# Seven-product up-projections summed in their PSUM banks, three down-products side by side, two plain pairs first

## Chip, cores and metric

The kernel runs on one core of a Trainium2 chip. The metric is the device time of one execution in microseconds (us); three executions of the kernel before gave 2522.79, 2525.11 and 2525.51, median 2525.11.

## What is computed

Two blocks of a transformer-like network on 512 tokens of width 1024, all in float32: sparse attention (A), a squared-ReLU MLP (M0), an RWKV-7 mixer (B), a second MLP (M1), a norm, a SwiGLU stage (S1), a convolution and mLSTM mixer (C), and a SwiGLU stage (S2). The change touches only M0 and M1:

```
def sqrelu_mlp(h, w_up, w_down):        # w_up 1024 x 4096, w_down 4096 x 1024
    u = jax.nn.relu(h @ w_up)
    return (u * u) @ w_down
...
x = x + sqrelu_mlp(rms_norm(x, mlp_norm[i]), mlp_w_up[i], mlp_w_down[i])
```

## The kernel before

Activations lie transposed: eight tiles of 128 features by 512 tokens (`self.x`). To keep float32 accuracy every operand is split in two: a rounded part `hi` (ScalarE, a cast) and the rest `lo` (VectorE, a subtraction), and every product is three matmuls, hi·hi, hi·lo and lo·hi (`mm3`, L452 to L456). A weight unit is 128 output features of 1024 inputs. `Weights` fetches raw tiles with SyncE's DMA queue (`wraw`, three buffers), and splits them in halves of 128 x 512 (`whi`, `wlo`). `ahead` splits as many halves as there are free buffers; a buffer is free once the products that used it have been written down, so the place of a call of `ahead` in the program settles what stands in ScalarE's and VectorE's queues at that point. Every engine works through its own queue in the order in which the program names the instructions (`manual_schedule`).

`mlp` (L568 to L626) goes through 32 blocks of hidden features in four groups of eight. A group first makes its eight blocks in four pairs (up-projection, ReLU times the norm's factor `rs`, square, split into `uh` and `ul`), then eight down-products, each over the group's eight blocks, each added to a tile of x (L624).

The first pair of all is plain: `product` with n=2, 48 matmuls of 512 columns in k = 0 to 7, six for each k. All other pairs are made by `product7` (L513): a Winograd form of Strassen's method on 2 x 2 blocks (two feature blocks by two halves of 256 tokens, the inputs in two halves of four tiles), with seven products P1 to P7 of 12 matmuls of 256 columns, 84 in all. Its inputs are P1, P2, P3 on the activations themselves and P4 to P7 on sums of them, made once for each MLP by `sums` (L485 to L511, four calls, q = 0 to 3). The sums of weights are made in place on VectorE (L170 to L177). The seven products of a pair lie in four of six PSUM banks, and ScalarE (L537) and VectorE (L538 to L545) join them into the four quarters of the output. The weights of a pair are split in the order P1, P7, P2, P6, P5, P3, P4, and the products run in that order too.

Beside the first plain pair run `stats_beside` (after k = 4 the sums of squares go through TensorE and the inverse root through ScalarE and VectorE; after k = 6 four transposes spread it, L436, and L438 copies it to `rs`) and the four calls of `sums` (after k = 1, 2, 3 and 5, L595 to L598).

Weight buffers: six halves for plain halves and P1, P2, P3 of the sevens, and six more for P4 to P7. In what follows the pairs of a group are called first to fourth.

## Time and profile before

| | |
|---|---|
| median of three runs | 2525.11 us |
| profiled execution, its own time | 2521.3 us |
| its span, first to last instruction | 2519.5 us |
| TensorE (PE) busy | 2307.1 us, 92% |
| VectorE (DVE) busy | 1610.8 us, 64% |
| ScalarE (ACT) busy | 1070.6 us, 42% |
| M0's products | from 274.0 to 668.1 us of the span |
| M1's products | from 1121.9 to 1517.9 us of the span |

In a timeline row stand the start in us, the duration, the engine, the line, the operation, the tiles out<-in with their shapes, and in brackets how long the engine was idle before and what ended that. PE's matmuls overlap, so the time one really takes is the distance to the next one's start. In a group's row stand the count, the busy time, the mean ns of one, and the idle time of the engine just before them. PEclk is the share of TensorE's clock that was granted.

### The profile page before, as it was taken

To read this page: it belongs to the slowest core of one execution; us is meant where nothing else is said; L and a number is where in the kernel's file an instruction comes from. 1 tells how busy PE (TensorE), PEld (TensorE's weight loads), DVE (VectorE), ACT (ScalarE), POOL (GpSimd) and SP (SyncE) were. 2 spreads that over 40 slices of the span, in tenths; PEclk is the share of its full clock that TensorE was granted. 3 is DMA by queue.
4 is the path that set the end of the run, shared out by engine and by line. 5 is a ranking of instruction groups with operands and counts; after the bars stand their busy time and mean duration, and the time that the engine had idled before them with its cause. 6 is when DMAs were issued, how large, how long until landed. Compare 5 with 4: busy or idle time off the path is not lost. (4 is left out here: it accounts for less than half of the span.)

```text
span 2519.5 us, 36278 instructions
## 1 busy us (share of the span) xinstructions
PE 2307.1 (92%) x13900; PEld 1930.3 (77%) x13900; DVE 1610.8 (64%) x2865; ACT 1070.6 (42%) x1967; POOL 424.9 (17%) x430
## 2 busy tenths in 40 slices
PE   7889788988988799887988989999998998999997
PEld 6668678878766676776878877888887787788886
DVE  7987757657688964777657665444457764634445
ACT  5566434334466365434334343333235544333222
POOL 3754000000355532220000020000012102100002
PEclk9999899999988898998999999999998999999999
DMA  4320222222323357532222222323222322222222
GB/s 157 94 80 19 70 89 93 89 87 86 119 64 118 101 169 204 164 101 68 92 84 92 93 84 93 100 92 101 92 74 74 111 76 76 92 92 93 100 95 65
DMA packets 105853, 241.97 MB, mean 96 GB/s; under 512 B 18120, under 2 KB 36936, under 8 KB 105680
## 3 DMA queue, kind: packets, MB, share of 16 engines
q1 hardware_dynamic: 103488, 234.46, 29.3%
q0 software_dynamic: 1040, 3.51, 0.4%
q8 instruction: 110, 1.80, 0.3%
q10 hardware_dynamic: 1152, 1.68, 0.2%
q14 instruction: 63, 0.52, 0.1%
HBM read 214.62 MB, written 19.22 MB: 93 GB/s over the span
## 5 line engine op out<-in xcount | busy, mean ns | idle before, releaser
L454 PE MATMUL mm<-xh,whi 128*128 128x512 f32 (+3 forms) x2080 | 742.9, 357 | 18.8 <-ACT whi L241 7.2
L456 PE MATMUL mm<-xh,wlo 128*128 128x512 f32 (+3 forms) x2080 | 733.6, 353 | 11.0 <-DVE wlo L242 11.0
L455 PE MATMUL mm<-xl,whi 128*128 128x512 f32 (+3 forms) x2080 | 734.1, 353 | 9.1 <-DVE xl L364 8.0
L242 DVE TENSOR_TENSOR wlo<-wraw,whi 128x512 fp32r<-128x512 f32 (+3 forms) x582 | 436.7, 769 | 405.7 <-ACT whi L241 404.5
L241 ACT CAST whi<-wraw 128x512 fp32r<-128x512 f32 (+2 forms) x601 | 355.1, 611 | 456.5 <-PE mm L455 398.0
L454 PEld LDWEIGHTS mm<-xh,whi 128*128 128x128 f32 (+2 forms) x2080 | 399.6, 192 | 78.0 <-issue 12.9
L456 PEld LDWEIGHTS mm<-xh,wlo 128*128 128x128 f32 (+2 forms) x2080 | 398.2, 191 | 66.7 <-DVE wlo L242 14.6
L455 PEld LDWEIGHTS mm<-xl,whi 128*128 128x128 f32 (+2 forms) x2080 | 399.4, 192 | 64.6 <-DVE xl L364 14.1
L454 PE MATMUL mm<-uh,whi 128*128 128x512 f32 (+1 forms) x900 | 356.0, 396 | 49.2 <-ACT uh L588 49.2
L455 PE MATMUL mm<-ul,whi 128*128 128x512 f32 (+1 forms) x900 | 355.3, 395 | 4.2 <-DVE ul L589 4.2
L456 PE MATMUL mm<-uh,wlo 128*128 128x512 f32 (+1 forms) x900 | 353.2, 392 | 0.0
L380 POOL TENSOR_TENSOR acc<-acc,sq 128x512 f32<-128x512 f32 (+1 forms) x55 | 73.5, 1337 | 1534.6 <-ACT sq L379 1534.2
L454 PEld LDWEIGHTS mm<-uh,whi 128*128 128x128 f32 x900 | 173.9, 193 | 90.4 <-ACT uh L588 52.7
L455 PEld LDWEIGHTS mm<-ul,whi 128*128 128x128 f32 x900 | 173.6, 193 | 47.1 <-DVE ul L589 9.2
L456 PEld LDWEIGHTS mm<-uh,wlo 128*128 128x128 f32 x900 | 173.5, 193 | 37.5
L230 ACT CAST whi<-wraw 128x512 fp32r<-128x512 f32 x180 | 107.3, 619 | 126.8 <-PE mm L455 43.2
L232 DVE TENSOR_TENSOR wlo<-wraw,whi 128x512 fp32r<-128x512 f32 x180 | 121.8, 686 | 26.0 <-ACT whi L230 23.7
L624 DVE TENSOR_TENSOR x<-mm,x 128x512 f32<-128x512 f32 x64 | 44.3, 691 | 69.8 <-PE mm L456 69.8
L589 DVE TENSOR_TENSOR ul<-u,uh 128x1024 fp32r<-128x1024 f32 x32 | 39.2, 1226 | 68.1 <-ACT uh L588 68.1
L587 ACT ACTIVATE u<-t 128x1024 f32<-128x1024 f32 x32 | 33.9, 1059 | 108.6 <-DVE t L610 102.8
L363 ACT ACTIVATE xh<-x,vec 128x512 fp32r<-128x512 f32 (+1 forms) x50 | 35.2, 705 | 87.3 <-DVE x L624 23.7
L772 ACT CAST uh<-a 128x512 fp32r<-128x512 f32 x44 | 27.3, 621 | 76.2 <-DVE a L771 76.2
(538 smaller groups left out, 3244.8 us busy)
## 6 DMA issues: line engine op xcount, KB each, us to landing
wraw<-in_ffn_in SPq DMA_DIRECT2D x88, 512.0 KB, 3.8
wraw<-in_up SPq DMA_DIRECT2D x64, 512.0 KB, 4.1
wraw<-in_down SPq DMA_DIRECT2D x64, 512.0 KB, 3.8
wraw<-in_rwkv SPq DMA_DIRECT2D x34, 512.0 KB, 4.9
wraw<-in_ffn_out SPq DMA_DIRECT2D x32, 512.0 KB, 3.7
wraw<-in_mix SPq DMA_DIRECT2D x32, 512.0 KB, 3.8
wraw<-in_dsa SPq DMA_DIRECT2D x23, 512.0 KB, 3.9
wraw<-in_ffn_out SPq DMA_DIRECT2D x16, 384.0 KB, 3.0
```

What stands on the lines that cost most here:

```text
L230: self.nc.scalar.copy(hi, t)
L232: self.nc.vector.tensor_sub(lo, t, hi.bitcast(F32))
L241: self.nc.scalar.copy(hi[:, :per], t)
L242: self.low.tensor_sub(lo[:, :per], t, hi[:, :per].bitcast(F32))
L363: nc.scalar.activation(hi, x, AF.Copy, scale=gm)
L380: (low or (nc.vector if m == NB - 1 else nc.gpsimd)).tensor_add(acc, acc, q[:, s])
L454: nc.tensor.matmul(ps, w[0], x[0], start=start, stop=False)
L455: nc.tensor.matmul(ps, w[0], x[1], start=False, stop=False)
L456: nc.tensor.matmul(ps, w[1], x[0], start=False, stop=stop)
L587: nc.scalar.activation(u, t, AF.Square)
L589: nc.vector.tensor_sub(lo, u, hi.bitcast(F32))
L624: nc.vector.tensor_add(self.x[m], p, self.x[m])
```

## The change

Three edits in M0 and M1.

1. `product7` now uses two PSUM banks and lets products go on in a bank in which others have been summed: the first half of bank a takes P1, then P6, P7 and P4 on top, bank x takes P2 in its first half and P5, then P3, in its second. ScalarE copies the sum out between (four copies, L535, L540, L543, L546 of the changed kernel), VectorE makes the rest (L608, L617) and the ReLUs (L600). The products run as P1, P2, P6, P5, P7, P3, P4; the weights are still split in the old order. The squares are made for each block of 128 x 512 by itself (L594, L595, L597).
2. The second pair of each MLP is plain too. Its `sums` run after k = 7 of the first pair (q = 0) and after k = 1, 3, 5 of the second.
3. The first three down-products of each group run side by side, three matmuls of each for every k.

```diff
--- before.py
+++ after.py
@@ -449,11 +449,11 @@
                 nc.vector.scalar_tensor_tensor(self.x[m], self.x[m], self.v(first, m), r1, op0=OP.mult, op1=OP.mult)
 
 
-    def mm3(self, ps, w, x, start, stop):
+    def mm3(self, ps, w, x, start, stop, **how):
         nc = self.nc
-        nc.tensor.matmul(ps, w[0], x[0], start=start, stop=False)
-        nc.tensor.matmul(ps, w[0], x[1], start=False, stop=False)
-        nc.tensor.matmul(ps, w[1], x[0], start=False, stop=stop)
+        nc.tensor.matmul(ps, w[0], x[0], start=start, stop=False, **how)
+        nc.tensor.matmul(ps, w[0], x[1], start=False, stop=False, **how)
+        nc.tensor.matmul(ps, w[1], x[0], start=False, stop=stop, **how)
 
     def product(self, xs, cols=128, n=1, pool=None, hook=None):
 
@@ -510,40 +510,49 @@
                           (("P5", 0, first), ("P4", 0, s), ("P6", 1, first), ("P7", 1, s))}
         return sums
 
-    def product7(self, xg, out):
+    def product7(self, xg, put):
 
 
         nc = self.nc
         at = self.w.get_seven()
-        banks = [self.mmp.tile([128, T], F32, name="mm") for _ in range(4)]
-        u2, u = self.c7.tile([128, 1, 256], F32, name="u2"), self.c7.tile([128, 2, 256], F32, name="u43")
+        a, x = (self.mmp.tile([128, T], F32, name="mm") for _ in range(2))
+        plus, c22 = (self.c7.tile([128, T], F32, name=n) for n in ("c1", "c2"))
         first, s = HALVES
-        P = dict(P1=banks[0][:, first], P2=banks[0][:, s], P6=banks[1][:, first], P5=banks[2][:, first],
-                 P7=banks[2][:, s], P3=banks[3][:, first], P4=banks[3][:, s])
-        two = [b.rearrange("p (i t) -> p i t", i=2) for b in banks]
-        C = out.rearrange("p (i t) -> p i t", i=4)
-        v = nc.vector
         self.w.ahead()
-        for p in SPLIT_ORDER:
+
+        def run(p, out, start):
+
             hi, lo = self.w.half(at[p])
             for q in range(NB // 2):
                 xs = {"P1": (q, first), "P2": (q + 4, first), "P3": (q + 4, s)}.get(p)
                 xs = [t[:, xs[1]] for t in xg[xs[0]]] if xs else self.x7[q][p]
                 c = slice(q * 128, (q + 1) * 128)
-                self.mm3(P[p], (hi[:, c], lo[:, c]), xs, q == 0, q == NB // 2 - 1)
+                self.mm3(out, (hi[:, c], lo[:, c]), xs, start and q == 0, q == NB // 2 - 1, skip_group_check=True)
             self.w.release(at[p])
-            if p == "P2":
-
-                nc.scalar.copy(u2[:, 0], P["P1"])
-                v.tensor_add(C[:, 0], u2[:, 0], P["P2"])
-            elif p == "P6":
-                v.tensor_add(u2[:, 0], u2[:, 0], P["P6"])
-            elif p == "P5":
-                v.tensor_add(u, u2.to_broadcast([128, 2, 256]), two[2])
-                v.tensor_add(C[:, 3], u[:, 1], P["P5"])
-            elif p == "P4":
-                v.tensor_add(C[:, 1:3], u, two[3])
-            self.w.ahead()
+
+        a, b, c = a[:, first], x[:, first], x[:, s]
+        run("P1", a, True)
+        nc.scalar.copy(plus[:, first], a)
+        self.w.ahead()
+        run("P2", b, True)
+        self.w.ahead()
+        run("P6", a, False)
+        nc.scalar.copy(plus[:, s], a)
+        self.w.ahead()
+        run("P5", c, False)
+        nc.scalar.copy(c22[:, first], c)
+        self.w.ahead()
+        run("P7", a, False)
+        nc.scalar.copy(c22[:, s], a)
+        put(1, 1, c22[:, first], c22[:, s])
+        self.w.ahead()
+        run("P3", c, False)
+        put(0, 0, x, plus)
+        self.w.ahead()
+        run("P4", a, False)
+        put(1, 0, a, None)
+        self.w.ahead()
+        put(2, 0, None, None)
 
     def part(self, p, w, c, x, s, k, K, free):
 
@@ -572,44 +581,63 @@
             self.stp = st.enter_context(tc.tile_pool(name="st_m", bufs=1, space=PSUM))
             self.sqp = st.enter_context(tc.tile_pool(name="sq_m", bufs=2))
             self.pad(st)
-            up = st.enter_context(tc.tile_pool(name="u_m", bufs=G // 2 + 1))
+            up = st.enter_context(tc.tile_pool(name="u_m", bufs=G + 2))
             self.pad(st)
-            tp = st.enter_context(tc.tile_pool(name="t_m", bufs=1))
+            tp = st.enter_context(tc.tile_pool(name="t_m", bufs=2))
             xg = self.xg
             st7 = ExitStack()
             sums = self.open_seven(st7)
 
-            def two():
-                return [tp.tile([128, 2 * T], F32, name=n) for n in "tu"]
-
-            def unit(t, u):
-                hi, lo = (up.tile([128, 2 * T], F32R, name=n) for n in ("uh", "ul"))
+            def square(t):
+                u = tp.tile([128, T], F32, name="u")
+                hi, lo = (up.tile([128, T], F32R, name=n) for n in ("uh", "ul"))
+                nc.scalar.activation(hi, t, AF.Square)
                 nc.scalar.activation(u, t, AF.Square)
-                nc.scalar.activation(hi, t, AF.Square)
-                nc.vector.tensor_sub(lo, u, hi.bitcast(F32))
-                us.extend((hi[:, i * T:(i + 1) * T], lo[:, i * T:(i + 1) * T]) for i in range(2))
+                us.append((hi, lo))
+                return lambda: nc.vector.tensor_sub(lo, u, hi.bitcast(F32))
+
+            def relu(t, p, s=ALL):
+                nc.vector.scalar_tensor_tensor(t[:, s], p, 0.0, self.rs[:, s], op0=OP.max, op1=OP.mult)
+
+            def put(i, h, p, plus):
+
+                if i == 2:
+                    later.pop()()
+                    return
+                if i and h:
+                    nc.vector.tensor_add(plus, p, plus)
+                    later.append(tp.tile([128, T], F32, name="t"))
+                    relu(later[0], plus, HALVES[1])
+                elif i:
+                    relu(later[0], p, HALVES[0])
+                    t, low = later
+                    later[:] = [square(t)]
+                    low()
+                else:
+                    nc.vector.tensor_add(plus, p, plus)
+                    t = tp.tile([128, T], F32, name="t")
+                    relu(t, plus)
+                    later.append(square(t))
 
             def beside(k):
                 self.stats_beside(k)
-                if k in (1, 2, 3, 5):
-                    sums(min(k - 1, 3), self.vec[:, VCOL[gn]:VCOL[gn] + NB], lambda: [t[:, :T] for t in two()])
+                if k == 7:
+                    sums_at(0)
+
+            def sums_at(q):
+                sums(q, self.vec[:, VCOL[gn]:VCOL[gn] + NB], lambda: [tp.tile([128, T], F32, name=n) for n in "tu"])
 
             for g in range(nff // G):
-                us = []
+                us, later = [], []
                 for f in range(0, G, 2):
-                    if g == 0 and f == 0:
-                        ps = self.product(xg, n=2, hook=beside)
-                        t, u = two()
-                        for i, p in enumerate(ps):
-                            nc.vector.scalar_tensor_tensor(t[:, i * T:(i + 1) * T], p, 0.0, self.rs,
-                                                           op0=OP.max, op1=OP.mult)
+                    if g == 0 and f < 4:
+                        ps = self.product(xg, n=2, hook=(beside, lambda k: k in (1, 3, 5) and sums_at(k // 2 + 1))[f // 2])
+                        for p in ps:
+                            t = tp.tile([128, T], F32, name="t")
+                            relu(t, p)
+                            square(t)()
                     else:
-                        t, u = two()
-                        self.product7(xg, t)
-                        t2 = t.rearrange("p (i t) -> p i t", i=2)
-                        nc.vector.scalar_tensor_tensor(t2, t2, 0.0, self.rs[:, None, :].to_broadcast([128, 2, T]),
-                                                       op0=OP.max, op1=OP.mult)
-                    unit(t, u)
+                        self.product7(xg, put)
                 last = g == nff // G - 1
                 if last:
                     self.w.close_seven()
@@ -619,8 +647,10 @@
                     self.xg_pool = None
                 if last and nxt:
                     blk = nxt()
+
+                ps = self.product(us, n=3)
                 for m in range(NB):
-                    p, = self.product(us)
+                    p = ps[m] if m < 3 else self.product(us)[0]
                     nc.vector.tensor_add(self.x[m], p, self.x[m])
                     if last and nxt:
                         blk(m)
@@ -2177,9 +2207,9 @@
     def f(aps):
         r = []
         for g in range(4):
-            r += [(aps[f"up{i}"][g * 4 + j], [1024, 1024], ["seven" if g + j else None] * 2) for j in range(4)]
+            r += [(aps[f"up{i}"][g * 4 + j], [1024, 1024], ["seven" if g or j > 1 else None] * 2) for j in range(4)]
             r += [(aps[f"down{i}"][g * 4 + j], [1024, 1024]) for j in range(4)]
-        return r, ([2] * 4 + [1] * 8) * 4
+        return r, ([2] * 4 + [3] + [1] * 5) * 4
     return f
 
 
```

The tables that follow show where instructions went. Names are those of the tiles; a number that tells two buffers apart is left in some.

**Beside the first plain pair, VectorE.** L497 to L506 are one call of `sums`, L389 to L399 the inverse root of the statistics, L438 the copy to `rs`. Before:

```order
L497 SCALAR_TENSOR_TENSOR t<-x_74,ng,t 128x256
L499 SCALAR_TENSOR_TENSOR u<-x_78,vec,t 128x512
L501 SCALAR_TENSOR_TENSOR t<-x_78,vec,u 128x256
L506 TENSOR_TENSOR xl_3081<-t,xh_3080 128x512
L506 TENSOR_TENSOR xl_3085<-u,xh_3084 128x512
L389 TENSOR_SCALAR sv<-st 128x4
L396 RECIPROCAL sy<-sy 128x4
L397 SCALAR_TENSOR_TENSOR stt<-sy,sv 128x4
L398 TENSOR_TENSOR stt<-stt,sy 128x4
L399 SCALAR_TENSOR_TENSOR sy<-stt,sy 128x4
L497 SCALAR_TENSOR_TENSOR t<-x_75,ng,t 128x256
```

Now:

```order
L242 TENSOR_TENSOR wlo<-wraw,whi 128x512 x3
L389 TENSOR_SCALAR sv<-st 128x4
L396 RECIPROCAL sy<-sy 128x4
L397 SCALAR_TENSOR_TENSOR stt<-sy,sv 128x4
L398 TENSOR_TENSOR stt<-stt,sy 128x4
L399 SCALAR_TENSOR_TENSOR sy<-stt,sy 128x4
L438 COPY rs<-st 128x512
L491 TENSOR_SCALAR ng<-vec 128x8
L497 SCALAR_TENSOR_TENSOR t<-x_72,ng,t 128x256
```

The inverse root stood behind three calls of `sums`; now it stands ahead of all four.

**Second plain pair to the first `product7` of an MLP, ScalarE, now.** L505 are the casts of the last call of `sums`, L594 and L595 the squares of the second plain pair, and L535 is the copy of P1 of the first `product7`:

```order
L496 ACTIVATE t<-x_75,vec 128x256
L505 CAST xh_3212<-t 128x512
L505 CAST xh_3216<-u 128x512
L594 ACTIVATE uh<-t 128x512
L595 ACTIVATE u<-t 128x512
L594 ACTIVATE uh<-t 128x512
L595 ACTIVATE u<-t 128x512
L230 CAST whi<-wraw 128x512
L230 CAST whi<-s_3255 128x512
L535 COPY c_3250<-mm 128x256
```

The copy comes next in that queue behind this piece, after one cast of `wraw` and one of `s`; before, no matmul waited for it.

**First to second pair of the second group, ScalarE.** L537 is the copy of P1 before, L535 now; L230 are casts of weights, L587 and L588, now L594 and L595, the squares of the first pair. Before:

```order
L537 COPY u_3883<-mm 128x256
L230 CAST whi<-wraw 128x512 x4
L230 CAST whi<-s_3979 128x512
L587 ACTIVATE u<-t 128x1024
L588 ACTIVATE uh<-t 128x1024
L230 CAST whi<-wraw 128x512 x2
L537 COPY u_4024<-mm 128x256
```

Now:

```order
L535 COPY c_3845<-mm 128x256
L540 COPY c_3845<-mm 128x256
L543 COPY c_3846<-mm 128x256
L546 COPY c_3846<-mm 128x256
L230 CAST whi<-wraw 128x512 x6
L594 ACTIVATE uh<-t 128x512
L595 ACTIVATE u<-t 128x512
L594 ACTIVATE uh<-t 128x512
L595 ACTIVATE u<-t 128x512
L230 CAST whi<-s_3943 128x512
L535 COPY c_3993<-mm 128x256
```

In both the copy of the second pair's P1 stands behind the squares of the first pair. Now it is also what P6, the third product of that pair, has to wait for, since P6 goes on in the bank of P1.

**The same place, VectorE.** L170 to L177 are sums of weights, L232 the `lo` parts. Before:

```order
L177 TENSOR_TENSOR wraw<-wraw,s_3856 128x512
L232 TENSOR_TENSOR wlo<-wraw,whi 128x512 x2
L538 TENSOR_TENSOR t<-u_3883,mm 128x256
L540 TENSOR_TENSOR u_3883<-u_3883,mm 128x256
L232 TENSOR_TENSOR wlo<-wraw,whi 128x512
L170 TENSOR_TENSOR wraw<-wraw 128x512
L232 TENSOR_TENSOR wlo<-wraw,whi 128x512
L542 TENSOR_TENSOR u_3884<-u_3883,mm 128x512
L543 TENSOR_TENSOR t<-u_3884,mm 128x256
L232 TENSOR_TENSOR wlo<-wraw,whi 128x512
L173 TENSOR_TENSOR s_3979<-wraw 128x512
L232 TENSOR_TENSOR wlo<-wraw,whi 128x512
```

Now (L608 and the L600 under it follow on P7 of the first pair, L617 and the L600 under it make the first block that the squares wait for):

```order
L608 TENSOR_TENSOR c_3846<-c_3846 128x256
L600 SCALAR_TENSOR_TENSOR t<-c_3846,rs 128x256
L177 TENSOR_TENSOR wraw<-wraw,s_3822 128x512
L232 TENSOR_TENSOR wlo<-wraw,whi 128x512 x3
L170 TENSOR_TENSOR wraw<-wraw 128x512
L232 TENSOR_TENSOR wlo<-wraw,whi 128x512 x2
L173 TENSOR_TENSOR s_3943<-wraw 128x512
L232 TENSOR_TENSOR wlo<-wraw,whi 128x512
L617 TENSOR_TENSOR c_3845<-mm,c_3845 128x512
L600 SCALAR_TENSOR_TENSOR t<-c_3845,rs 128x512
L600 SCALAR_TENSOR_TENSOR t<-mm,rs 128x256
L597 TENSOR_TENSOR ul<-u,uh 128x512
```

Nine instructions on weights, for the second and the third pair, now stand in one run between the first pair's P7 and L617; before, they were spread over its products.

## Rows read from the trace of the kernel before

**Rows 1.** The page: engines (busy, share, count), and one costly group.

```profile
PE 2307.1 (92%) x13900; PEld 1930.3 (77%) x13900; DVE 1610.8 (64%) x2865; ACT 1070.6 (42%) x1967; POOL 424.9 (17%) x430
...
L454 PE MATMUL mm<-uh,whi 128*128 128x512 f32 (+1 forms) x900 | 356.0, 396 | 49.2 <-ACT uh L588 49.2
```

**Rows 2.** Windows: us, busy (count) of PE, PEld, DVE, ACT, POOL; PEclk, DMA share, GB/s.

```profile
284.70:298.00 13.30, 0.00 (x1) 0.03 (x1) 10.93 (x23) 7.49 (x14) 0.00 (x0) 0.66 0.15 49
425.70:430.00 4.30, 4.30 (x19) 3.15 (x18) 2.78 (x5) 3.31 (x6) 0.00 (x0) 1.00 0.00 1
430.00:436.10 6.10, 0.02 (x1) 0.00 (x0) 3.84 (x6) 1.99 (x3) 0.00 (x0) 0.68 0.50 172
436.10:442.00 5.90, 5.37 (x12) 3.94 (x13) 3.12 (x4) 1.14 (x3) 0.00 (x0) 0.50 0.00 0
442.00:480.00 38.00, 38.00 (x164) 30.78 (x163) 19.71 (x31) 11.61 (x19) 0.00 (x0) 0.99 0.30 98
480.00:520.20 40.20, 40.20 (x337) 40.20 (x336) 32.38 (x52) 16.75 (x28) 0.00 (x0) 1.00 0.28 92
1132.60:1145.40 12.80, 0.03 (x1) 0.00 (x0) 10.83 (x23) 6.14 (x13) 0.00 (x0) 0.61 0.15 52
```

**Rows 3.** Timeline of PE: first matmuls of MLPs and groups, transposes, two at half clock.

```profile
273.99 0.47 PE L454 MATMUL mm<-xh,whi 128*128 128x512 f32 x1 [0.88 <-DVE x L1078]
...
298.00 0.44 PE L436 MATMUL st<-con,sy 128*128 128x128 f32 x1 [13.31 <-DVE sy L399]
...
301.44 0.41 PE L454 MATMUL mm<-xh,whi 128*128 128x256 f32 x1
...
301.65 0.41 PE L455 MATMUL mm<-xl,whi 128*128 128x256 f32 x1
...
385.43 0.28 PE L454 MATMUL mm<-xh,whi 128*128 128x256 f32 x1
...
573.49 0.28 PE L454 MATMUL mm<-xh,whi 128*128 128x256 f32 x1
...
1121.90 0.47 PE L454 MATMUL mm<-xh,whi 128*128 128x512 f32 x1 [0.88 <-DVE x L2169]
...
1234.27 0.28 PE L454 MATMUL mm<-xh,whi 128*128 128x256 f32 x1
...
1423.14 0.28 PE L454 MATMUL mm<-xh,whi 128*128 128x256 f32 x1
```

**Rows 4.** Timeline of DVE beside M0's first pair.

```profile
281.88 0.48 DVE L497 SCALAR_TENSOR_TENSOR t<-x,ng,t 128x256 f32<-128x256 f32 x1
...
285.71 0.49 DVE L497 SCALAR_TENSOR_TENSOR t<-x,ng,t 128x256 f32<-128x256 f32 x1
...
296.25 0.15 DVE L389 TENSOR_SCALAR sv<-st 128x4 f32<-128x4 f32 x1
...
297.69 0.16 DVE L399 SCALAR_TENSOR_TENSOR sy<-stt,sy 128x4 f32<-128x4 f32 x1
...
301.45 0.69 DVE L438 COPY rs<-st 128x512 f32<-128x512 f32 x1
```

**Rows 5.** Timeline of ACT, first to third pair of M0's third group, which begins at 480.00.

```profile
494.24 1.06 ACT L587 ACTIVATE u<-t 128x1024 f32<-128x1024 f32 x1 [2.84 <-DVE t L610]
...
495.20 1.04 ACT L588 ACTIVATE uh<-t 128x1024 fp32r<-128x1024 f32 x1
...
498.66 0.36 ACT L537 COPY u<-mm 128x256 f32<-128x256 f32 x1
...
498.93 1.14 ACT L230 CAST whi<-wraw 128x512 fp32r<-128x512 f32 x2
...
502.86 0.62 ACT L230 CAST whi<-wraw 128x512 fp32r<-128x512 f32 x1 [0.58 <-DMA wraw<-in_up]
```

**Rows 6.** Timeline of DVE in the first pair of the same group.

```profile
489.04 0.42 DVE L543 TENSOR_TENSOR t<-u,mm 128x256 f32<-128x256 f32 x1
...
489.38 0.69 DVE L232 TENSOR_TENSOR wlo<-wraw,whi 128x512 fp32r<-128x512 f32 x1
...
491.18 0.68 DVE L545 TENSOR_TENSOR t<-u,mm 128x512 f32<-128x512 f32 x1
...
491.78 0.69 DVE L175 TENSOR_TENSOR wraw<-s,wraw 128x512 f32<-128x512 f32 x1
...
492.38 0.69 DVE L232 TENSOR_TENSOR wlo<-s,whi 128x512 fp32r<-128x512 f32 x1
...
496.28 1.23 DVE L589 TENSOR_TENSOR ul<-u,uh 128x1024 fp32r<-128x1024 f32 x1 [2.07 <-ACT uh L588]
```

**Rows 7.** Timeline of SyncE's DMA queue in the same group.

```profile
498.73 0.54 SPq L186 DMA_DIRECT2D wraw<-in_up  x1
```

## Prediction

> **What bounds the kernel now.** I read the page first: TensorE is busy 92% of the span, and one group of matmuls, the first of the down-products, has 49.2 us of idle time before it, ended by ScalarE's `uh` [rows 1]. Then the windows of M0 and M1, to see how PE fares inside a group. Four `product7` in a row leave no gap: 336 matmuls in 40.2 us at full clock, 0.120 us each, 1.44 us a product, 10.05 us a pair (window 480.00 to 520.20 [rows 2]). The down-products run at 38.0 us for 164 matmuls, 0.232 us each, so 192 take 44.5 us. Between them PE stands still: 18 matmuls on the first six blocks, then 6.1 us of nothing while VectorE and ScalarE make the last pair's squares, then 5.9 us at half the granted clock (windows from 425.70 to 442.00 [rows 2]). The starts of the groups give the whole loss: the second to third groups of M0 take 573.49 - 385.43 = 188.06 us, those of M1 188.87 [rows 3], on average 94.2 a group. Work is 40.2 + 44.5 = 84.7, so 9.5 us are lost in each later group: 6.1 idle, 0.5 for the first `ul`, 2.9 for the clock.
>
> The first group of each MLP loses more. PE waits 13.3 us before the transposes of the statistics (298.00 [rows 3]), 12.8 in M1 [rows 2]; the inverse root ends at 297.69 [rows 4] because three calls of `sums`, 3.83 us each (L497 to L497), stand ahead of it. These groups take 385.43 - 273.99 = 111.4 and 1234.27 - 1121.90 = 112.4 us [rows 3].
>
> What the reader should look at last is ScalarE. In the third group the second pair starts at 480.00 + 10.05 = 490.05, so its P1 ends at 491.5. The copy of that P1, L537, runs at 498.66 [rows 5], 7.2 us later, behind the squares (494.24 and 495.20), which waited for VectorE. Nobody minds: P6 has a bank of its own there.
>
> **The change part by part.**
>
> *Three down-products side by side.* The last blocks of `us` are wanted after 54 matmuls instead of 18, 12.5 us after the start. The queues worked out below have the last `ul` ready 4.6 us after the fourth pair ends. The tail goes: -9.5 us in each of eight groups, clock included. Its weights are no new wait: the three halves of the second k-half are split by then too.
>
> *Second pair plain.* 48 x 0.232 = 11.1 us instead of 10.05: +1.1 us, twice. It loads the same two raw tiles, so SyncE's queue carries as many transfers as before; only the moments at which they are issued change, and the one that matters is in the chain below.
>
> *Statistics ahead of `sums`.* Freed of what stood ahead, the root takes from 296.25 to 297.85, 1.6 us [rows 4]; k = 5 and 6 last 12 x 0.232 = 2.8 us, and the `lo` parts issued after k = 3 are done before. The 13.3 us wait goes. What is late next is counted below.
>
> *VectorE's work.* 512-column operations follow each other at 0.60 us (491.18, 491.78, 492.38), 256-column ones at 0.34 (489.04 to 489.38) [rows 6]. A `product7` pair now costs 11 on weights + add, ReLU and two `ul` (4 x 0.60) + three of 256: 6.6 + 2.4 + 1.0 = 10.0 us, 2 us less than before and just PE's 10.05.
>
> *The new wait.* P6 goes on in P1's bank, so it must wait for the copy L535, and that copy stands behind the previous pair's squares. I follow the listed queues from the end of P7 of the first pair, with 0.05 us for a handover.
> - ScalarE copies P7's sum (0.37), VectorE adds and takes the ReLU (0.42 each): 1.35.
> - L177 and the `lo` of P5: 0.60 + 0.69, so 2.65. Only now is a raw buffer free and SyncE fetches the second tile of the third pair's weights. Such a load was issued at 498.73 [rows 7] and its cast began at 502.86 [rows 5]: 4.1 us, so 6.8. The five operations between (3.0 us) fit beside it.
> - L173, a `lo`, L617, ReLU: 0.60 + 0.60 + 0.74 + 0.69 = 9.4.
> - ScalarE: four squares of 512 columns, a cast and the copy. I give a square the pace of a cast, 0.52 (two in 1.14 us [rows 5]), a little over half of the 0.96 from the one 1024-column square to the next: 4 x 0.52 + 0.52 + 0.37 and two handovers, 12.55.
>
> PE has P3, P4, and the next P1 and P2 in the meantime, 5.75 us. It stands still for **6.8 us**, and since the next pair's VectorE work begins with its P7, the chain closes: pair after pair. Second to third pair the same, 6.8. Third to fourth, the burst holds two halves of down-weights, of which one waits for the same load (6.8, cast and `lo` to 8.1), then L617 and ReLU 9.5, two squares 10.6, a cast and `lo` of a further half ahead of the last ReLU 12.35, squares and copy 13.9: **8.1 us** idle. The first pair of a group meets empty queues and waits for nothing.
>
> Each of these waits is as long as the 6.1 us after which the clock stood at 0.50 [rows 2], so each also costs the 2.9 us above. The Trainium skill ("TensorE: Matmul & The Clock Gate", section "HAM oscillation — how this bites in real kernels") tells of a loop that goes to the low clock at every wait, with 1.67 us throttled a turn, that is 0.84 lost. By that figure the 22 restarts after the change would cost 18 us instead of 64 and the time would be 2624. The rows here show the larger price.
>
> Later groups: 84.7 + 6.8 + 6.8 + 8.1 + 3 x 2.9 = 115.1, against 94.2: +20.9, six times, **+125**.
>
> *First groups.* k = 0 to 6 end 298.00 - 13.31 - 273.99 = 10.7 us in [rows 3], as before. On VectorE then come: `rs` 0.7 and the first call of `sums` with its small operation 4.0, two blocks of ReLU, squares and `ul` that wait for each other 4.9 (0.69 + 2 x 0.52 + 0.69 each, with handovers), nine operations on weights 5.5, `sums` 3.85, five on weights 3.0, two `sums` 7.7, two blocks 4.9, and L173 with the cast and the copy 1.7: 36.2 us to the copy of the first `product7`'s P1, begun 0.6 us in. PE has transposes, k = 7, the plain pair, P1 and P2: 0.5 + 1.4 + 11.1 + 2.9 = 15.9. It stands still 20.9 us there. The whole group: 10.7 + 15.9 + 20.9 + 7.2 (P6 to P4) + 10.05 + 8.1 + 2 x 2.9 + 44.5 = 123.2, against 111.9: **+11**, twice.
>
> Sum: 125 + 22 = +147 on the profiled execution's 2521.3 gives 2668; the median is 3.8 above that execution, so about 2670.
>
> *Bounds.* The trace has no matmul that waits for a copy. If the 22 restarts (three in each later group, two in each first) cost no clock, 64 us come off, and if loads never hold the queues, another 1 us at each of 12 places and 2 at eight: 2578. If the clock stays low through P7 as well (12 matmuls at the 0.21 of 301.44 to 301.65 [rows 3] instead of 0.12: +1.1) and the chain is a tenth longer (1.3), 22 times: 2723. I take the rows' values, since the wait is like the one they show.
>
> **The rivals.**
>
> *A. The copies are in time (faster).* Then the bank only costs its own 0.37 us copy, which lies beside the next product. Later groups 84.7 (-9.5, six times), first groups 88.4 (-23.5, twice): -104, 2421. The point that decides is 1.44 us from P1's end to the end of the copy. For it: the first pair of every group does so. Against it: 7.2 us at 498.66 [rows 5], with a queue in the same order as now. The Trainium skill ("TensorE: Matmul & The Clock Gate", section "Loop structure matters more than you think") has copying a result out of PSUM leave the matmuls dense, the next turn's following at once; by that rule it would be 2421. The trace agrees only as long as the next matmul writes another bank. 6%.
>
> *B. Only the first stretch holds.* VectorE's 10.0 us fits PE's 10.05; if its queue ran beside PE with no chain, later groups lose 1 us instead of 9.5 (-51), and the first groups keep the 20.9 and one restart: 88.4 + 23.8 = 112.2, no change. 2474. Against it: the four squares and the burst are in queues that start with P7. 4%.
>
> [...] 4%.
>
> **How the numbers follow.** Forecast 86%, A 6, B 4, C 4. Change of over 0.2% (5 us, what a measurement here can tell from none): faster by A and B 10%, slower by the forecast and C, less 2% for a draw: 88%. The range for 8 in 10, 2590 to 2715, is the forecast's own, a little inside the bounds above, since both ends take two unlikely things at once.
>
> **What would show it.** Right: PE idle some 7 us before the third product of second, third and fourth pairs, ended by ScalarE's L535, with the granted clock at 0.50 after it; the 49.2 us before `uh` gone; the gap before L436 gone and one of about 20 us before the first `product7`'s P6. Wrong: pairs at 10 us without gaps, L535 within 1.4 us of P1's end, or waits that end on VectorE or a DMA instead.

## The result, and the profile after

The changed kernel takes 2661.4 us (median of four runs, 2659.23 to 2669.24) against 2524.88: a ratio of 1.0548, 95% interval 1.0525 to 1.057. Forecast were 2670, in a range from 2590 to 2715. The profiled execution took 2659.23 us, with a span of 2657.3.

The page of the changed kernel: engines, and the two groups that answer to [rows 1].

```profile
PE 2328.1 (88%) x13828; PEld 1958.0 (74%) x13828; DVE 1576.2 (59%) x2847; ACT 1104.9 (42%) x2107; POOL 426.7 (16%) x430
...
L454 PE MATMUL mm<-xh,whi 128*128 128x512 f32 (+4 forms) x2056 | 763.4, 371 | 209.4 <-ACT c L535 142.2
...
L454 PE MATMUL mm<-uh,whi 128*128 128x512 f32 (+1 forms) x900 | 347.5, 386 | 0.0
```

The 49.2 us before `uh` are gone. In their place PE waits 142.2 us for one line, L535, the copy of P1's sum. The view of that line says how often:

```profile
who waited for it (us, times):
...
  PE mm L454: 142.2, 20
```

Twenty waits of 7.1 us on average: three in each of six later groups, one in each first group. The third group of M0 by windows (columns as in [rows 2]); the stretches without PE are those between P2 and P6 of the second, third and fourth pair:

```profile
510.32:523.35 13.03, 13.03 (x109) 12.88 (x107) 5.87 (x11) 4.30 (x9) 0.00 (x0) 1.00 0.12 38
523.35:530.04 6.69, 0.06 (x1) 0.00 (x1) 4.76 (x9) 3.58 (x7) 0.00 (x0) 0.72 0.23 86
530.04:541.60 11.56, 11.56 (x84) 11.42 (x84) 6.03 (x11) 3.92 (x8) 0.00 (x0) 0.87 0.13 40
541.60:548.39 6.79, 0.07 (x2) 0.01 (x1) 4.77 (x9) 3.58 (x7) 0.00 (x0) 0.88 0.25 90
548.39:560.90 12.51, 12.51 (x84) 12.37 (x84) 4.96 (x9) 3.30 (x7) 0.00 (x0) 0.79 0.14 44
560.90:568.64 7.74, 0.07 (x1) 0.00 (x1) 3.89 (x7) 3.73 (x8) 0.00 (x0) 0.69 0.19 65
568.64:578.30 9.66, 9.66 (x61) 9.66 (x62) 3.77 (x7) 2.10 (x5) 0.00 (x0) 0.72 0.31 110
578.30:623.08 44.78, 44.78 (x194) 36.02 (x193) 24.72 (x40) 15.67 (x26) 0.00 (x0) 1.00 0.28 94
```

21.2 us idle; 84 matmuls that take 11.56 and 12.51 us where [rows 2] had 84 in 10.05, at a granted clock of 0.87 and 0.79 on average; and down-products without a gap, 44.78 us. The 11.56 us begin with 13 matmuls mostly 0.21 us apart, at a clock of 0.50 (1.2 GHz), and go on at 0.12 us and 1.00 (2.4 GHz). What stands ahead of the copy is seen on ScalarE (timeline, first of these waits):

```profile
524.32 0.62 ACT L230 CAST whi<-wraw 128x512 fp32r<-128x512 f32 x1 [1.49 <-DMA wraw<-in_up]
527.02 0.63 ACT L594 ACTIVATE uh<-t 128x512 fp32r<-128x512 f32 x1 [2.09 <-DVE t L600]
...
528.60 0.61 ACT L595 ACTIVATE u<-t 128x512 f32<-128x512 f32 x1
529.12 0.60 ACT L230 CAST whi<-s 128x512 fp32r<-128x512 f32 x1
529.63 0.36 ACT L535 COPY c<-mm 128x256 f32<-128x256 f32 x1
```

A cast that waits for a load, squares that wait for VectorE's ReLU, a cast, the copy. PE goes on 0.41 us after the copy's start (timeline of PE):

```profile
530.04 0.58 PE L454 MATMUL mm<-xh,whi 128*128 128x256 f32 x1 [6.63 <-ACT c L535]
```

In the first group the wait for the statistics, 13.31 us in [rows 3], is gone, and the first `product7` stands still before its P6 (timeline of PE, M0):

```profile
285.76 0.60 PE L436 MATMUL st<-con,sy 128*128 128x128 f32 x4
...
322.62 0.55 PE L454 MATMUL mm<-xh,whi 128*128 128x256 f32 x1 [21.12 <-issue]
...
343.00 0.58 PE L454 MATMUL mm<-xh,whi 128*128 128x256 f32 x1 [7.60 <-ACT c L535]
```

"issue" only says that the profile names no releaser. ScalarE's timeline has the copy just ahead of 322.62, so it is the same wait:

```profile
319.66 0.61 ACT L595 ACTIVATE u<-t 128x512 f32<-128x512 f32 x1
...
321.63 0.62 ACT L230 CAST whi<-s 128x512 fp32r<-128x512 f32 x1 [0.85 <-DVE s L173]
322.16 0.36 ACT L535 COPY c<-mm 128x256 f32<-128x256 f32 x1
```

One thing was not forecast. The stage after an MLP starts later than before; PE's first matmul there, after M0 and after M1:

```profile
739.26 0.76 PE L454 MATMUL mm<-xh,whi 128*128 128x512 f32 x1 [3.44 <-DVE x L654]
...
1652.69 0.77 PE L454 MATMUL mm<-xh,whi 128*128 128x512 f32 x1 [5.71 <-DVE x L654]
```

Before, these waits were 2.25 and 0.88 us.

**Where the time came from**, a first group counted from PE's first matmul to the end of its last, a later one from the end of the group ahead to its own end. First groups: 111.6 and 112.5 before, 122.5 and 120.7 now, +19. Later groups: on average 94.3 before, 113.1 now, +18.8 six times, +113. Ends of the MLPs: +6. The stretches outside M0 and M1 cancel: -5.2 between them (451.6, now 446.4), +3.9 behind, +1.2 ahead. Sum +138, and the spans differ by 137.8.

### The profile page after: what moved, and what is told of

Same layout as the page of the kernel before. It is cut to its first block, busy times and chain, and to the rows that moved or that the text cites. A ratio compares the mean times of both kernels' runs of the same rounds, so it can differ in the third digit from the quotient of the medians.

```text
span 2657.3 us, 36157 instructions
## 1 busy us (share of the span) xinstructions
PE 2328.1 (88%) x13828; PEld 1958.0 (74%) x13828; DVE 1576.2 (59%) x2847; ACT 1104.9 (42%) x2107; POOL 426.7 (16%) x430
## 5 line engine op out<-in xcount | busy, mean ns | idle before, releaser
L454 PE MATMUL mm<-xh,whi 128*128 128x512 f32 (+4 forms) x2056 | 763.4, 371 | 209.4 <-ACT c L535 142.2
L455 PE MATMUL mm<-xl,whi 128*128 128x512 f32 (+4 forms) x2056 | 750.7, 365 | 10.8 <-DVE xl L364 9.5
L456 PE MATMUL mm<-xh,wlo 128*128 128x512 f32 (+4 forms) x2056 | 747.6, 364 | 9.0 <-DVE wlo L242 9.0
L242 DVE TENSOR_TENSOR wlo<-wraw,whi 128x512 fp32r<-128x512 f32 (+2 forms) x590 | 438.4, 763 | 443.6 <-ACT whi L241 430.9
L454 PEld LDWEIGHTS mm<-xh,whi 128*128 128x128 f32 (+3 forms) x2056 | 416.6, 203 | 273.6 <-ACT c L535 146.3
L241 ACT CAST whi<-wraw 128x512 fp32r<-128x512 f32 (+3 forms) x609 | 360.5, 611 | 456.6 <-PE mm L455 388.1
L455 PEld LDWEIGHTS mm<-xl,whi 128*128 128x128 f32 (+3 forms) x2056 | 416.8, 203 | 66.9 <-DVE xl L364 15.0
L456 PEld LDWEIGHTS mm<-xh,wlo 128*128 128x128 f32 (+3 forms) x2056 | 414.9, 202 | 65.4 <-DVE wlo L242 11.8
L230 ACT CAST whi<-wraw 128x512 fp32r<-128x512 f32 x168 | 99.3, 619 | 101.6 <-DMA wraw<-in_up 25.6
L232 DVE TENSOR_TENSOR wlo<-wraw,whi 128x512 fp32r<-128x512 f32 x168 | 112.8, 688 | 12.7 <-ACT whi L230 8.9
L608 DVE TENSOR_TENSOR c<-c 128x256 f32<-128x256 f32 x28 | 11.9, 425 | 169.4 <-ACT c L546 169.4
L594 ACT ACTIVATE uh<-t 128x512 fp32r<-128x512 f32 x64 | 40.1, 627 | 90.5 <-DVE t L600 90.5
L597 DVE TENSOR_TENSOR ul<-u,uh 128x512 fp32r<-128x512 f32 x64 | 44.1, 688 | 30.2 <-ACT u L595 30.2
```

The costliest lines, as they stand in the source:

```text
L230: self.nc.scalar.copy(hi, t)
L232: self.nc.vector.tensor_sub(lo, t, hi.bitcast(F32))
L241: self.nc.scalar.copy(hi[:, :per], t)
L242: self.low.tensor_sub(lo[:, :per], t, hi[:, :per].bitcast(F32))
L454: nc.tensor.matmul(ps, w[0], x[0], start=start, stop=False, **how)
L455: nc.tensor.matmul(ps, w[0], x[1], start=False, stop=False, **how)
```

## The experiments

The runs of the kernel before beside these have medians of 2522 to 2523 us. The table has the mean of the six later groups and the two first groups, counted as above, in the profiled execution.

| run | median us | ratio to before (95%) | later group | first groups |
|---|---|---|---|---|
| before | 2524.88 | | 94.3 | 111.6, 112.5 |
| changed | 2661.4 | 1.0548 (1.0525 to 1.057) | 113.1 | 122.5, 120.7 |
| e1 | 2630.45 | 1.0429 (1.0414 to 1.0445) | 109.8 | 117.5, 119.0 |
| e2 | 2514.19 | 0.9967 (0.9956 to 0.9979) | 92.3 | 110.3, 110.0 |
| e8 | 2474.70 | 0.9813 (0.9797 to 0.9829) | 86.5 | 104.8, 104.0 |
| e3 | 2608.84 | 1.0347 (1.0331 to 1.0362) | 105.2 | 117.2, 118.4 |
| e10 | 2561.89 | 1.0154 (1.0137 to 1.0171) | 98.5 | 115.5, 114.2 |
| e7 | 2471.31 | 0.9800 (0.9783 to 0.9817) | 86.4 | 109.3, 109.2 |
| e5 | 2631.84 | 1.0435 (1.0417 to 1.0454) | 107.2 | 122.8, 118.6 |
| e4 | 2507.88 | 0.9948 (0.9933 to 0.9963) | 92.4 | 106.4, 106.1 |
| e6 | 2446.08 | 0.9699 (0.9683 to 0.9715) | 86.6 | 90.0, 90.0 |
| e11 | 2520.57 | 0.9996 (0.9986 to 1.0005) | 98.3 | 96.7, 95.6 |
| e9 | 2448.29 | 0.9709 (0.9695 to 0.9722) | 86.4 | 95.7, 96.4 |
| e12 | 2434.95 | 0.9653 (0.9640 to 0.9667) | 86.4 | 90.3, 90.4 |

### What are the side-by-side products worth?

**e1, the changed kernel without them.**

```diff
-                ps = self.product(us, n=3)
...
-                    p = ps[m] if m < 3 else self.product(us)[0]
+                    p = self.product(us)[0]
...
-        return r, ([2] * 4 + [3] + [1] * 5) * 4
+        return r, ([2] * 4 + [1] * 8) * 4
```

> The changed kernel, but the first three down-products of a group run one after the other as before. Theory: the tail of the groups was taken away twice, once by the side-by-side order and once because the squares now come block by block; the last ul is ready 4.6 us after P4 and would be wanted 4.9 us after it, so this costs 0 to 1 us in each of eight groups, and the clumped adds at the end of each MLP go, which gives some 5 us back: 2655 to 2668, and no PE gap over 1.5 us inside the down-products. Rival: the side-by-side order itself carries the 9.5 us a group of the prediction: 2661 + 76 = 2737, with 6 us gaps before uh back in the profile.

Measured 2630.45: 31 us less than the changed kernel, and below the range. As expected the down-products have no gap, and the waits at the ends are 2.04 and 0.88 us again. What the theory had missed lies ahead of them: the fourth pair waits 4.94 us instead of 7.6. ScalarE in the changed kernel's fourth pair:

```profile
558.23 0.61 ACT L241 CAST whi<-wraw 128x512 fp32r<-128x512 f32 x1
561.73 0.62 ACT L241 CAST whi<-wraw 128x512 fp32r<-128x512 f32 x1 [2.88 <-DMA wraw<-in_down]
564.43 0.63 ACT L594 ACTIVATE uh<-t 128x512 fp32r<-128x512 f32 x1 [2.08 <-DVE t L600]
```

and in e1:

```profile
548.62 1.14 ACT L241 CAST whi<-wraw 128x512 fp32r<-128x512 f32 x2
552.09 0.63 ACT L594 ACTIVATE uh<-t 128x512 fp32r<-128x512 f32 x1 [2.33 <-DVE t L600]
```

Side by side, the first halves of three weight units are split first; the second comes from a tile that is only just being fetched. One by one, both halves of the first tile come first.

**e2, the kernel before with the side-by-side products alone.** (The same lines of `mlp` and of the groups, the other way round.)

> The kernel before with the side-by-side down-products alone. Theory: each of eight groups loses its tail of 9.5 us (6.1 idle, 0.5, 2.9 clock) because the last ul, 11.8 us after the group's last product, is wanted only at 12.5 us: 2525 - 76 = 2449, with no gap before uh. If the chain to ul is a little longer than the 12.5 us, a gap of 1 us stays in some groups: up to 2460. Rival: the three halves of the second k-half of the weights come late instead and PE waits for them: 2500 or more. At the end of an MLP the three adds come in a clump, as in the changed kernel: up to 5 us lost there.

Measured 2514.19, 8 us less instead of 76. That lies in the rival's range, but PE waits for a bank and not for weights: it stops after six matmuls of the down-products (timelines of ScalarE, VectorE and PE of e2):

```profile
521.86 0.36 ACT L537 COPY u<-mm 128x256 f32<-128x256 f32 x1
...
523.22 0.41 DVE L538 TENSOR_TENSOR t<-u,mm 128x256 f32<-128x256 f32 x1
...
523.69 0.80 PE L454 MATMUL mm<-uh,whi 128*128 128x512 f32 x1 [4.51 <-DVE t L538]
```

The pair takes four of six banks and three products want three: the third gets the bank of P1 and P2, which L538 reads, behind the late copy L537. The late copy that cost nobody anything [rows 5] costs as soon as anybody wants that bank.

**e8, e2 with a seventh bank.**

```diff
-            self.mmp = st.enter_context(tc.tile_pool(name="mm_m", bufs=6, space=PSUM))
+            self.mmp = st.enter_context(tc.tile_pool(name="mm_m", bufs=7, space=PSUM))
```

> The kernel before with the side-by-side down-products (as in the run e2) and a seventh PSUM bank for the products. Theory: in e2 the third of the three products stood still for 4.5 us because its bank was the P1 and P2 bank of the fourth pair, whose reader L538 stands behind that pair's late copy of P1; with a seventh bank it takes a free one, and the last ul comes at 11.8 us where it is wanted at 12.5: 2522 - 76 = 2446, plus up to 5 for clumped adds at the ends, 2445 to 2465, and no gap over 1.5 us in the down-products. Rival: with the bank free, PE just waits for uh or ul of the last pair instead, for 3 us or more: 2490 to 2515.

Measured 2474.7, 10 us above the range. The 4.5 us are gone, so the bank was the cause; what is left is a wait of 0.76 us for `ul` in each group, and up to 0.7 for `uh`. A later group gets back 7.8 of the 9.5 us (94.3, now 86.5). The rest of the miss lies outside the groups: the ends wait 3.48 and 5.70 us, and the stretches between and behind the MLPs are 3.9 us longer each.

### Is it the bank or what stands ahead of the copy?

**e3, the squares behind the next pair's copy of P1.**

```diff
         nc.scalar.copy(plus[:, first], a)
+        put(2, 0, None, None)
         self.w.ahead()
...
         put(1, 0, a, None)
         self.w.ahead()
-        put(2, 0, None, None)
...
                 if i == 2:
-                    later.pop()()
+                    for low in [square(t) for t in ready]:
+                        low()
+                    ready.clear()
                     return
...
-                    t, low = later
-                    later[:] = [square(t)]
-                    low()
+                    ready.append(later.pop())
...
-                    later.append(square(t))
+                    ready.append(t)
...
```

> The changed kernel with the four squares of a pair moved in ScalarE's queue behind the next pair's copy of P1, and their ul parts behind that on VectorE; nothing else moves. Theory: the copy then waits only for the casts of the weights, the last of them behind the raw tile's load, some 8.3 us after the end of P7 where PE wants it at 5.75: idle before P6 falls from 6.7 to about 2.5 us (7.6 to about 3.5 in the fourth pair), 0.8 us may come back before P7 because the squares now stand ahead of the copy of P6, and part of the clock's price goes. Later groups 95 to 100 us instead of 113.6: 2535 to 2575, likeliest 2555. Rival 1: VectorE is the bound of a pair, and the wait only moves to P7: later groups stay over 108, total over 2630. Rival 2: it is the bank itself (the handover from ScalarE to PE) that costs, not what stands ahead of the copy: idle before P6 stays over 5 us.

Measured 2608.84, 53 us less than the changed kernel but 34 above the range. Most of the waits, 6.7 us and more before, are now some 4.05 us. It didn't fall to 2.5 because the copy met another wait that the squares had covered (ScalarE and VectorE of e3):

```profile
527.40 0.69 DVE L600 SCALAR_TENSOR_TENSOR t<-c,rs 128x512 f32<-128x512 f32 x1
...
528.21 0.37 ACT L535 COPY c<-mm 128x256 f32<-128x256 f32 x1 [1.36 <-DVE t L600]
```

The copy writes `c1`, of which there is one buffer, and the last pair's ReLU, behind the burst on VectorE, still reads it: it ends at 528.09, and the copy begins at 528.21. A second buffer comes with e7; it was not tried alone.

**e10, the burst spread out instead** (run after e7, whose 2471 us its expectation names): e1, with one half of weights split after each product and none at the start of a pair (lines move up by one: the copy is L534, the ReLU L599, the squares L593 and L594).

```diff
-        self.w.ahead()
...
         nc.scalar.copy(plus[:, first], a)
-        self.w.ahead()
+        self.w.ahead(1)
         run("P2", b, True)
-        self.w.ahead()
+        self.w.ahead(1)
...
```

> The changed kernel without the side-by-side products (as e1), with one half of weights split after each of the seven products instead of a burst after P7; the squares stay where the change put them, c1 and c2 stay in one buffer. Theory: the burst alone made the copy late. Counted from P3's end: L617 and ReLU 1.5, two squares 2.6, the second ReLU by 2.5, its squares 3.7, a cast and the copy 4.6, where PE wants it at 4.3: gaps of 0.3 to 1 us, later groups 86 to 88, total as e7: 2471, range 2460 to 2495. Rival: the squares ahead of the copy cost too, as moving them in e3 gave 52 us: gaps of 2 to 3 us and a slower clock, 2520 or more.

Measured 2561.89; the rival was right. The waits fall from 6.6 us (4.9 in the fourth pair) to between 2.9 and 3.2, and behind most of them the clock is at 0.50. ScalarE of e10:

```profile
416.96 0.60 ACT L230 CAST whi<-wraw 128x512 fp32r<-128x512 f32 x1
418.66 0.63 ACT L593 ACTIVATE uh<-t 128x512 fp32r<-128x512 f32 x1 [1.09 <-DVE t L599]
419.20 0.61 ACT L594 ACTIVATE u<-t 128x512 f32<-128x512 f32 x1
419.71 0.60 ACT L230 CAST whi<-wraw 128x512 fp32r<-128x512 f32 x1
420.22 0.36 ACT L534 COPY c<-mm 128x256 f32<-128x256 f32 x1
```

With no burst left, the second ReLU, its squares and a cast are still ahead of the copy.

**e7, both, and two buffers for `c1` and `c2`**: e3's squares and e10's `ahead(1)` without the side-by-side products, and

```diff
-        self.c7 = st.enter_context(tc.tile_pool(name="c7", bufs=1))
+        self.c7 = st.enter_context(tc.tile_pool(name="c7", bufs=2))
...
-            up = st.enter_context(tc.tile_pool(name="u_m", bufs=G + 2))
+            up = st.enter_context(tc.tile_pool(name="u_m", bufs=G + 1))
```

> The changed kernel without the side-by-side products (as e1), with the squares behind the next pair's copy of P1 (as e3), the tiles c1 and c2 in two buffers (in e3 the copy waited for the ReLU that reads c1), ten blocks of u cut to nine to make room, and one half of weights split after each of the seven products instead of a burst after P7. Theory: what costs in the changed kernel is the order of the queues, not the bank: now nothing but the squares and at most three casts of weights that are there stands ahead of a copy, so the pairs run without gaps over 1 us: later groups 85 to 88 us instead of 109.4 in e1, first groups lose only the wait of the fourth pair: 2630 - 6 x 23 - 2 x 6 = 2480, range 2465 to 2510. Rival: VectorE, with 10.0 us of work a pair, becomes the bound and gaps of 2 us or more stay: over 2530.

Measured 2471.31: 2.0% (1.8 to 2.2) under the kernel before, 159 us less than e1. ScalarE and PE of e7, and then one of its groups by windows, up- and down-products:

```profile
568.19 0.37 ACT L534 COPY c<-mm 128x256 f32<-128x256 f32 x1 [1.24 <-PE mm L456]
568.46 0.64 ACT L593 ACTIVATE uh<-t 128x512 fp32r<-128x512 f32 x1
...
572.96 0.38 PE L454 MATMUL mm<-xh,whi 128*128 128x256 f32 x1 [0.50 <-ACT c L540]
```

```profile
469.97:511.70 41.73, 40.73 (x337) 40.33 (x336) 32.46 (x57) 24.66 (x51) 0.00 (x0) 1.00 0.29 97
511.70:556.50 44.80, 44.80 (x194) 36.04 (x193) 25.32 (x40) 15.05 (x25) 0.00 (x0) 1.00 0.28 98
```

The copy of P1 now waits for PE and not PE for the copy; 1.00 us is left idle in 41.73, at a clock of 1.00. That is what going on in a bank still costs: in two pairs of the group P7 waits 0.5 us for the next copy, L540, of the sum with P6, which stands behind a cast. What stood ahead of the copies in two queues cost 23 us a group (109.8 in e1, 86.4 here).

### What does the clock cost?

**e5, the changed kernel with its idle time filled.** P2's matmuls are repeated four times into a bank of their own.

```diff
-        a, x = (self.mmp.tile([128, T], F32, name="mm") for _ in range(2))
+        a, x, idle = (self.mmp.tile([128, T], F32, name="mm") for _ in range(3))
...
-            for q in range(NB // 2):
+            for q in [*range(NB // 2)] * (5 if out is b and self.fill else 1):
+                n += 1
...
-                self.mm3(out, (hi[:, c], lo[:, c]), xs, start and q == 0, q == NB // 2 - 1, skip_group_check=True)
+                self.mm3(out if n <= 4 else idle[:, first], (hi[:, c], lo[:, c]), xs, start and q == 0, q == NB // 2 - 1, skip_group_check=True)
...
+                        self.fill = f > 0
                         self.product7(xg, put)
```

> The changed kernel with 48 more matmuls of 256 columns (P2 repeated four times into a bank of its own that nobody reads) between P2 and P6 of every second, third and fourth pair; the output does not change. They take 48 x 0.12 = 5.8 us, so they fit into the idle time of 6.7 to 7.6 us and PE is busy through it. Theory: the wait itself is unchanged and only the clock's price goes: the groups' sums in the changed kernel's trace leave 2.4 us a restart, so 2661 - 20 x 2.4 = 2613. By the 2.9 us of the prediction: 2603. By the Trainium skill's 0.84 (TensorE: Matmul & The Clock Gate, HAM oscillation): 2644. Rival: idle time does not lower the clock here, or the extra matmuls delay the chain: 2661 or more.

Measured 2631.84, 30 us less with 1056 matmuls more, and 19 more than expected. The third group of M0 by windows:

```profile
503.72:565.65 61.93, 58.31 (x482) 57.68 (x480) 34.12 (x58) 24.54 (x50) 0.00 (x0) 1.00 0.21 69
565.65:610.45 44.80, 44.80 (x195) 36.04 (x194) 24.80 (x40) 15.66 (x26) 0.00 (x0) 1.00 0.29 94
```

The wait is the same: 3 x 5.8 us filled and 3.6 idle are 21.0, against 6.63 + 6.71 + 7.67 = 21.0. The clock is 1.00 throughout, and the group takes 106.7 us instead of 112.8: 2.0 us for each restart after some 7 us of idle time. Over the six later groups the mean falls by 5.9, 35 us in all; the stretches outside the MLPs took some 9 us more than in the changed kernel, which is why the total shows less. 2.0 lies between the 2.9 of the prediction and the 0.84 of the Trainium skill (TensorE: Matmul & The Clock Gate, HAM oscillation).

### What is best?

**e4, the four-bank form in the changed kernel**: `product7`, its joins and the 1024-column squares are those of before; the second plain pair, the moved `sums` and the side-by-side products stay.

> The changed kernel with the four-bank seven-product form and joins of the kernel before (second plain pair, moved sums and side-by-side down-products kept). Theory: all of the loss lies in the bank, so the later groups take 85 us (40.2 + 44.5) and the first groups lose the 13.3 us wait for the statistics but still stand still for about 14 us at their first seven-product pair, since VectorE has the four calls of sums ahead of its weights: 105 us a first group. 2525 - 6 x 9.5 - 2 x 6.5 = 2455, range 2440 to 2470. Rival: the plain second pair or the moved sums cost on their own, first groups above 115: 2475 or more.

Measured 2507.88, 38 us above the range. No pair waits any more in the later groups, so the loss did lie in the two-bank form as it was queued; but they come to 92.4 and not 85, since e2's wait for the bank, 4.52 us, is back, with the clock at 0.50 behind it. In the first groups PE waits 11.2 us for the casts of three calls of `sums` (xh, L505).

**e6, with seven banks and four plain pairs in the first group.**

```diff
-                    if g == 0 and f < 4:
-                        ps = self.product(xg, n=2, hook=(beside, lambda k: k in (1, 3, 5) and sums_at(k // 2 + 1))[f // 2])
+                    if g == 0:
+                        ps = self.product(xg, n=2, hook=beside if f == 0 else lambda k: k == 3 and sums_at(f // 2))
...
-            r += [(aps[f"up{i}"][g * 4 + j], [1024, 1024], ["seven" if g or j > 1 else None] * 2) for j in range(4)]
+            r += [(aps[f"up{i}"][g * 4 + j], [1024, 1024], ["seven" if g else None] * 2) for j in range(4)]
```

> e4 with seven PSUM banks for the products and the whole first group of each MLP plain (four plain pairs, one call of sums beside each). Theory: later groups 85 us instead of 94.2 (-55 in six), first groups 10.7 + 1.9 + 3 x 11.1 + 44.5 = 90.4 instead of 111.9 (-43 in two), +6 for clumped adds at the ends: 2522 - 92 = 2430, range 2415 to 2450. Rival: PE waits beside the plain pairs, since VectorE has 8.7 us of work in 11.1, or the side-by-side products still wait 3 us a group: 2455 or more.

Measured 2446.08. The first groups take 90.0 us, as worked out: two more plain pairs than in e4, at some 1.1 us each, cost less than the wait for `sums`. Later groups as in e8.

**e11 and e9, the same edit in e10 and in e7.**

> e10 with the whole first group of each MLP plain, one call of sums beside each of its pairs. Theory: the 19 to 21 us before the first seven-product pair's P6 is VectorE's queue of sums, weights and blocks, and goes when these lie beside plain pairs: first groups 90 us (as in e6) instead of 109: 2471 - 2 x 19 = 2433, range 2420 to 2450, under e6's 2446 because the adds at the ends of the MLPs are not clumped. Rival: the wait only moves to the first seven-product pair of the second group, 5 us or more there: 2445 or more.

> e7 with the whole first group of each MLP plain, as in e11. Theory: the same 19 us go from each first group: 2471 - 38 = 2433, range 2420 to 2450; within 8 us of e11 either way, since moving the squares on top of spreading the weights changes only gaps of half a us. Rival: with the squares behind the copy the last ul of a group comes later and PE waits 1 us or more in the down-products: 10 us above e11.

Measured 2520.57 and 2448.29. The pair differs by what e10 and e7 do in the later groups, 98.3 against 86.4, and not by 8 us at most: e11's range and the 8 us rested on e10's pairs being free of waits, which they were not. e9 is inside its range, at the upper end. In both the first groups take some 96 us, 6 above e6: after a plain fourth pair PE waits four times for `uh` and `ul`, in e9 1.23, 0.75, 0.52 and 0.75 us.

**e12, e9 with the side-by-side products in the first group alone.**

```diff
+                ps = self.product(us, n=3) if g == 0 else []
                 for m in range(NB):
-                    p = self.product(us)[0]
+                    p = ps[m] if m < len(ps) else self.product(us)[0]
...
-        return r, ([2] * 4 + [1] * 8) * 4
+        return r, [2] * 4 + [3] + [1] * 5 + ([2] * 4 + [1] * 8) * 3
```

> e9 with the first three down-products side by side in the first group of each MLP alone. Theory: after a plain fourth pair the squares come at once and one behind the other, so PE waits for uh and ul four times in e9 (1.2 + 0.75 + 0.5 + 0.75 us and some clock), which 54 matmuls instead of 18 cover; the first groups go from 95.6 to 90 us, the ends of the MLPs stay unclumped: 2448 - 11 = 2437, range 2430 to 2445, faster than both kernels and than e6. Rival: the three halves of the side-by-side order hold the queues ahead of the second group as they did in the changed kernel: no gain, 2448 or more.

Measured 2434.95 us, 3.5% under the kernel before and the fastest of all. M0's first group and the two halves of its second, by windows:

```profile
275.20:365.34 90.14, 90.05 (x396) 73.38 (x397) 56.25 (x95) 39.41 (x70) 0.00 (x0) 1.00 0.28 95
365.34:407.08 41.74, 40.75 (x337) 40.34 (x336) 33.94 (x60) 24.97 (x52) 0.00 (x0) 1.00 0.28 97
407.08:451.88 44.80, 44.80 (x194) 36.05 (x193) 25.32 (x40) 15.05 (x25) 0.00 (x0) 1.00 0.29 99
```

The three parts of the change all stand in it: products summed in two banks, plain pairs at first, three down-products side by side where PE would wait for the last squares. No run shows that summing in two banks is faster by itself: e6, with four banks a pair out of seven, has later groups of 86.6 us against 86.4.

## Why the prediction was right, and where it was not

- **The new wait: right.** Forecast 6.8, 6.8 and 8.1 us; measured 6.63, 6.71 and 7.67 in the group shown. Place, releaser (L535) and what stands ahead of it are as followed through the queues: the load, L173, the ReLUs, four squares, a cast. e3, e10 and e7 show that it is these and not the bank: with both the burst and the squares out of the way it is gone. What is left, 0.5 us twice a group in e7, is before P7.
- **The first `product7`: right.** 20.9 forecast, 21.12 and 21.23 measured; the wait for the statistics went as forecast.
- **The clock: the term was too large.** 2.9 us a restart, from one stretch behind a wait of 6.1 us at 512 columns; e5 gives 2.0. That is some 16 us too much over the 18 restarts of the later groups, which came out 12 us below the forecast together; the waits were 3 us shorter in all, and the groups' work was longer than the 84.7 us put down for it (e7's 86.4 hold 1.0 of idle time). The Trainium skill's 0.84 was too small for this kernel; with it the forecast would have been 2624.
- **Three down-products side by side, "-9.5 us in each of eight groups": the effect came, but not by this part.** e1 has no gap in the down-products without it, and is 31 us faster. What takes the tail away instead came with edit 1, the joins and squares by block, in which the last `ul` starts 4.2 us after the first down-product in e1 and 2.8 in e7; before it was 10.5 (425.66 to 436.14). Kernel before (the copy of P1 of the group's last pair, 1.9 us after its P4 ended at 425.66, and the last `ul`), then the last `ul` of e1 and of e7:

```profile
427.60 0.36 ACT L537 COPY u<-mm 128x256 f32<-128x256 f32 x1
...
436.14 1.23 DVE L589 TENSOR_TENSOR ul<-u,uh 128x1024 fp32r<-128x1024 f32 x1 [2.13 <-ACT uh L588]
```

```profile
569.22 0.69 DVE L597 TENSOR_TENSOR ul<-u,uh 128x512 fp32r<-128x512 f32 x1 [0.62 <-ACT u L595]
```

```profile
514.51 0.69 DVE L596 TENSOR_TENSOR ul<-u,uh 128x512 fp32r<-128x512 f32 x1 [0.35 <-ACT u L594]
```

  Before, the joins of the last pair stood behind that late copy; now P6 can't begin before its copy, so none is late behind P4. In e7 all four squares stand behind the whole pair, so it isn't only that the first block's are queued after P3. The late copy, the joins and the width of the squares were not tried apart, so their shares stay open. That the total held although the gain was credited to the wrong part is luck. In the changed kernel the side-by-side order only costs: 3.4 us in each later group, most of it in the fourth pair, and clumped adds at the ends. "Its weights are no new wait" was the sentence that failed. The prediction had those halves and their load in its 8.1 us, but charged them to the bank.
- **"Nobody minds": true only of the kernel before.** e2 took the same late copy's bank for another product and lost 4.5 us a group.
- **Ends of the MLPs: missed, +6 us.** All seven kernels whose last group has three products side by side (the changed one, e2, e3, e4, e5, e6, e8) wait 5.7 us at M1's end; before, e1, e7, e9, e10, e11 and e12 wait 0.88. So it belongs to that order; why it comes to 5 us was not followed further.
- **Rival A** had 84.7 us for the later groups, and e7 and e12 have 86.4: with the copy ready 0.4 us after P1's end the pairs are dense but for the 1.0 us above, as the Trainium skill has it (TensorE: Matmul & The Clock Gate, "Loop structure matters more than you think"). In these runs that held only where nothing long stood ahead of the copy in its engine's queue; in the changed kernel the copy began 7.7 us after P1's end (529.63, P1 ending at 521.9), and the rule alone would have given the wrong sign.

The errors partly cancel: -12 in the later groups, -3 in the first, +6 at the ends make 138 of the 147 forecast.

## What to carry to other kernels

Before two results share a bank, or a bank is given to somebody else, follow the queue of the engine that empties it: a copy of 0.36 us that costs nothing today is on the path the moment a matmul waits for it, and everything queued ahead of it comes along. Preparation for later pairs belongs in small steps between the instructions that others wait for, not in one run wherever buffers happen to come free. And when a change has several parts, credit a gain to a part only after asking whether another part gives it already: here the part to which 76 us were credited cost 31.
